# Negated blocks of h made in pieces from SBUF, and a given engine order behind the attention

## The chip, the cores and the metric

The kernel runs on one core of one Trainium2 chip. The metric is the device time of one execution in microseconds; three runs of the kernel before gave 793.66, 793.96 and 795.17, median 793.96. Engines are called as in the profile: PE multiplies matrices, DVE, ACT and POOL do elementwise work, and SP issues most DMA transfers (SPq); POOL issues the DMA transfers that add into DRAM.

## The reference

One decoder layer on 16 meta tokens and 1024 tokens, width 1024, all in fp32:

```python
h = rmsnorm(x, norm_g)                        # x with the meta tokens ahead: 1040 rows
u_pool, z_pool, q, k, v, z_attn, f_logit, g_pool, g_attn = split(h @ w_in)
y_pool = causal_multiscale_pool(u_pool, pool_w, pool_scale) * silu(z_pool)
y_attn = forgetting_attention(q, k, v, log_sigmoid(f_logit + b_forget)) * silu(z_attn)
merged = sigmoid(g_pool) * (y_pool @ w_up_pool) + sigmoid(g_attn) * (y_attn @ w_up_attn)
out = rmsnorm(x + merged @ w_out, final_norm_g)     # meta rows dropped
```

Attention has 8 heads of 64, causal, with a decay by the running sum of the log forget gates. Pooling has four groups of 128 channels with trailing means over 2, 4, 8 and 16 positions.

## The kernel before

**Precision.** Each fp32 operand is split into a high and a low part (`hh` and `hl` of h, `whi` and `wlo` of weights): ACT copies the high part, DVE or POOL subtracts it. A product is three matmuls: high by high, low by high, high by low.

**Stages** (times of the profiled execution, about): norm, transposes and the first projections to 54 us, gates to 88; sixteen attention units (four pairs of heads, two heads each, two halves of the queries) to 513; seven products for the gates z (0 to 6, `g_prod`, L932) from 527 to 620; the up projections (L164 again) to 707; the output product (L1148) to the end.

**In the attention** PE also computes the remaining projections in chunks of 128 columns of `w_in` (`split_w`, `w_chunk`, L164). A chunk's weights, 512 KB, are loaded by SP into a tile "raw" of pool `wp` (L145), which holds two such tiles in turn; ACT copies `whi` (L150), POOL subtracts `wlo` (L152). PE takes its instructions in a written order, so a chunk that is not ready holds up everything behind it.

**Sums for the products.** The two gates z take seven products of 512-blocks instead of eight (a Strassen-like scheme), from sums of weight blocks (GS) and of blocks of h (HS), and the output product takes sums TD of w_out. They are made in DRAM while attention runs, by the table `SUMS`: behind unit i stands a list of steps. `put` is a plain DMA on SP, `add` an adding DMA on POOL's queue. `put_neg` (L590 to L595) makes the negative of a block of h: in two halves it loads the block from DRAM into tiles "neg" *of the ring "raw"*, ACT negates them there (L594), and SP stores them (L595).

**Behind the attention** the products take turns in two sets of four PSUM banks (`ga_`, `gb_`). Their operands are loaded by `w_in_` (weights, tiles "graw") and `h_in` (blocks of h, "hraw") and split by `w_split` (ACT and POOL, L912 and L136) and `h_split` (ACT and DVE, L921 to L925). `keep` copies a bank (ACT), `plus_` adds a bank to what is there (DVE, L947) and applies silu (ACT, L944). Between them lie `pool_chain` (running sums of the pooling, DVE, from a tile "u" loaded from DRAM), `pool_split` (tiles plh and pll), `attn_in` (the attention's output y from DRAM), `attn_norm` (L841 and L842: reciprocal sums "rc" broadcast from DRAM, y times rc) and `pool_mm` (the small matmuls of pooling). Here PE's order is written by hand, while ACT, DVE, POOL and SP get theirs from the scheduler. Pool `gp` holds 13 tiles "g" in rotation: u, its running sums, plh, pll, y and rc all come from it, and a tile's first writer waits for the last reader of what lay in that place.

Of the kernel before, what the change touches and what calls it, by code (L numbers as in the profile page):

```python
# [54 lines left out]
def tile_hybrid_block(ctx, tc, x, meta, norm_g, w_in, b_forget, pool_w, pool_scale,  # L55
# [344 lines left out]
    grow = ap_.tile([1, D], F32, name="grow", tag="t")  # L400
# [166 lines left out]
    HS = {n: dr.tile([512, 512], F32, name=f"hs{n}") for n in ("11", "12", "21", "22", "n12", "n21", "A", "B", "C", "X")}  # L567
# [22 lines left out]
    def put_neg(n):  # L590
        for k in range(2):
            t = wp.tile([128, 2, 512], F32, name="neg", tag="raw")
            put(t, rows_of(HS[n])[:, 2 * k:2 * k + 2])
            after(nc.scalar.activation(t, t, AF.Copy, scale=-1.0), exps[-1])  # L594
            nc.sync.dma_start(rows_of(HS["n" + n])[:, 2 * k:2 * k + 2], t)  # L595

    SUMS = {
        0: [(put_h, "21"), (put_h, "12")],
        1: [(add_h, "21"), (put, GS[1], GB["11"])],
        2: [(add_h, "12"), (put, GS[3], GB["12"])],  # L600
        3: [(put_neg, "21"), (add, GS[1], GB["12"])],
        4: [(put, TD[1], WB["11"]), (put, TD[3], WB["12"]), (add, GS[3], GB["22"])],
        5: [(put_neg, "12"), (put_h, "11")],
        6: [(add, TD[1], WB["12"]), (add_h, "11"), (put, GS[2], GS[3])],
        7: [(add, TD[3], WB["22"]), (put_h, "22"), (put, HS["X"], HS["n21"])],
        8: [(add_h, "22"), (add, rows_of(HS["X"]), rows_of(HS["11"]))],
        9: [(put, TD[2], TD[3]), (put, HS["A"], HS["22"]), (add, GS[2], GB["11"])],
        10: [(add, TD[2], WB["11"]), (add, rows_of(HS["A"]), rows_of(HS["n21"]))],
        11: [(put, HS["B"], HS["A"]), (put, GS[4], GS[2])],
        12: [(put, TD[4], TD[2]), (add, rows_of(HS["B"]), rows_of(HS["11"])), (add, GS[4], GB["21"])],  # L610
        13: [(add, TD[4], WB["21"]), (put, HS["C"], HS["B"])],
        14: [(add, rows_of(HS["C"]), rows_of(HS["n12"]))],
# [203 lines left out]
    def pool_mm(g):  # L816
# [3 lines left out]
        for c0, c1 in HALVES:  # L820
# [31 lines left out]
    def pool_chain(g):  # L852
# [7 lines left out]
        while step < win:  # L860
# [6 lines left out]
            i += 1  # L867
# [85 lines left out]
    for p in range(3):  # L953
        attn_in(p)
# [313 lines left out]
```

## Time and profile before

| What | us |
|---|---|
| median of three runs | 793.96 |
| the profiled execution, as timed | 793.09 |
| its span in the trace | 791.4 |
| PE busy in the span | 730.7 |
| mean granted clock of PE (share of full) | 0.968 |

All rows shown below are of this one execution. "Idle before" is the time in which an engine stood still before a group of instructions, with what ended it; waits of an engine that is not the limit cost nothing. The granted clock is the share of its full clock at which PE was allowed to run in a stretch.

### The profile page before, as it was taken

What the parts mean: (1) busy time and instruction counts of PE and PEld (TensorE: products, weight loads), DVE (VectorE), ACT (ScalarE), POOL (GpSimd) and SP (SyncE); (2) the same over time, 40 slices, a digit from 0 to 9 for tenths busy, and PEclk for the clock granted to TensorE, in tenths of its full rate; (3) what the DMA queues carried; (4) which work ended last, traced back from release to release, by engine and by line L of the source; (5) the groups of instructions that cost most, each with busy time, mean ns of one, the idle gap of its engine ahead of it and who ended that gap; (6) DMA issues with size and microseconds to landing.
All of it is one profiled execution on the core that took longest, in us unless ns stands there. A gap on an engine that the chain in (4) does not pass through costs nothing.

```text
span 791.4 us, 10759 instructions
## 1 busy us (share of the span) xinstructions
PE 730.7 (92%) x3637; PEld 620.7 (78%) x3637; DVE 554.0 (70%) x1023; ACT 398.3 (50%) x814; POOL 340.2 (43%) x404
## 2 busy tenths in 40 slices
PE   8999999997498849998899998997899999999996
PEld 6988899985397648897888876785688888888885
DVE  5643788797189648798887886945548845687774
ACT  7744555555255535575465643524457522524354
POOL 5331238462315245654274645733678401004343
PEclk9999999999599979999999999999799999999999
DMA  9111127918910794847928877289740536764005
GB/s 299 41 28 46 45 83 192 253 33 184 263 35 15 212 263 98 231 91 180 198 64 212 216 179 187 62 276 315 216 147 16 224 107 234 257 241 133 0 1 213
DMA packets 91241, 120.44 MB, mean 152 GB/s; under 512 B 11041, under 2 KB 54049, under 8 KB 91058
## 3 DMA queue, kind: packets, MB, share of 16 engines
q1 hardware_dynamic: 81440, 100.36, 40.4%
q0 software_dynamic: 8448, 16.78, 12.6%
q10 hardware_dynamic: 1298, 2.63, 0.9%
q8 instruction: 28, 0.46, 0.2%
q14 instruction: 27, 0.22, 0.1%
HBM read 92.28 MB, written 52.63 MB: 183 GB/s over the span
## 4 chain that ended last, share of the span: by engine, by line
PE 68%; DMA 9%; DVE 8%; ACT 5%; issue 3%; POOL 1%; SPq 0%; POOLq 0%; DVEq 0%; ACTq 0%
PE pj L164 41%; PE pj L1148 8%; PE pj L932 7%; PE po L718 3%; DMA raw<-in_w_in_dram 3%; PE pt L932 2%; PE pt L1148 2%; DMA hsn<-neg 2%; PE ps L657 2%; PE ps L658 2%; ACT S L666 1%; DVE pl L702 1%; DVE m L673 1%; DMA rc<-recs 1%; DMA sp_u<-st 1%
## 5 line engine op out<-in xcount | busy, mean ns | idle before, releaser
L164 PE MATMUL pj<-hh,whi 128*128 128x512 f32 (+3 forms) x640 | 149.1, 360 | 31.8 <-ACT whi L150 28.7
L164 PEld LDWEIGHTS pj<-hh,whi 128*128 128x128 f32 x640 | 110.2, 192 | 45.2 <-ACT whi L150 29.6
L164 PE MATMUL pj<-hl,whi 128*128 128x512 f32 (+3 forms) x640 | 145.5, 354 | 0.0
L152 POOL TENSOR_TENSOR wlo<-raw,whi 128x256 fp32r<-128x256 f32 x116 | 92.7, 886 | 119.3 <-ACT whi L150 61.7
L164 PE MATMUL pj<-hh,wlo 128*128 128x512 f32 (+3 forms) x640 | 143.0, 350 | 0.0
L164 PEld LDWEIGHTS pj<-hl,whi 128*128 128x128 f32 x640 | 109.8, 191 | 12.1
L164 PEld LDWEIGHTS pj<-hh,wlo 128*128 128x128 f32 x640 | 108.4, 188 | 11.9
L702 DVE TENSOR_TENSOR pl<-S,ph 128x512 fp32r<-128x512 f32 (+4 forms) x112 | 88.6, 806 | 15.5 <-ACT ph L701 14.9
L710 POOL TENSOR_TENSOR acc<-acc,S 128x272 f32<-128x272 f32 (+4 forms) x80 | 76.1, 952 | 13.6 <-ACT S L698 8.9
L666 ACT ACTIVATE S<-ps,negc 128x400 f32<-128x400 f32 (+2 forms) x96 | 49.1, 517 | 57.4 <-DVE S L664 54.9
L136 POOL TENSOR_TENSOR gw<-graw,gw 128x256 fp32r<-128x256 f32 x48 | 50.6, 1089 | 39.6 <-ACT gw L912 17.2
L673 DVE TENSOR_TENSOR m<-m,S 128x272 f32<-128x272 f32 (+4 forms) x80 | 48.0, 601 | 26.8 <-ACT S L666 25.3
L698 ACT ACTIVATE S<-S 128x512 f32<-128x512 f32 (+4 forms) x112 | 49.7, 479 | 31.4 <-DVE S L697 31.2
L150 ACT ACTIVATE whi<-raw 128x512 fp32r<-128x512 f32 x58 | 34.2, 623 | 41.0 <-DMA raw<-in_w_in_dram 28.9
L701 ACT ACTIVATE ph<-S 128x512 fp32r<-128x512 f32 (+4 forms) x112 | 51.9, 479 | 1.8 <-PE po L718 1.4
L932 PE MATMUL pj<-gh,gw 128*128 128x512 f32 x180 | 45.8, 411 | 7.5 <-ACT gh L921 6.1
L697 DVE TENSOR_TENSOR S<-S,pt 128x512 f32<-128x512 f32 (+4 forms) x112 | 51.5, 496 | 0.8
L932 PEld LDWEIGHTS pj<-gh,gw 128*128 128x128 f32 x180 | 35.6, 200 | 16.8 <-ACT gh L921 7.3
L657 PE MATMUL ps<-qa,ka 128*128 128x512 f32 (+4 forms) x112 | 38.8, 347 | 7.8 <-ACT S L666 7.3
L1040 DVE TENSOR_TENSOR rl<-pj,rl 128x512 f32<-128x512 f32 x32 | 22.1, 689 | 31.3 <-PE pj L164 31.3
L718 PE MATMUL po<-pl,V 128*128 128x512 f32 (+4 forms) x112 | 38.7, 345 | 3.6 <-DVE pl L702 3.4
L658 PE MATMUL ps<-ql,ka 128*128 128x512 f32 (+4 forms) x112 | 38.3, 342 | 0.0
(227 smaller groups left out, 1325.9 us busy)
## 6 DMA issues: line engine op xcount, KB each, us to landing
raw<-in_w_in_dram SPq DMA_DIRECT2D x31, 512.0 KB, 6.2
xt<-in_x_dram SPq DMA_DIRECT2D x8, 512.0 KB, 6.7
hs<-hh SPq DMA_DIRECT2D x4, 1024.0 KB, 8.6
hs<-hl POOLq DMA_DIRECT2D x4, 1024.0 KB, 10.5
sp_gp<-st SPq DMA_DIRECT2D x16, 256.0 KB, 4.4
gs<-in_w_in_dram POOLq DMA_DIRECT2D x4, 1024.0 KB, 11.5
td<-in_w_out_dram POOLq DMA_DIRECT2D x4, 1024.0 KB, 10.9
sp_ga<-st SPq DMA_DIRECT2D x16, 256.0 KB, 2.7
```

The costliest lines, as they stand in the source:

```text
L152: ins = nc.gpsimd.tensor_tensor(lo[:, k:k + 2], raw[:, k:k + 2], r32(hi[:, k:k + 2]), op=ALU.subtract)
L164: nc.tensor.matmul(ps, a, b, start=(i == 0), stop=(i == len(seq) - 1))
L657: nc.tensor.matmul(ps[:kb, c0:], ka[:, k0:k0 + kb], qa[:, q0 + c0:q0 + 512], start=True, stop=False)
L658: nc.tensor.matmul(ps[:kb, c0:], ka[:, k0:k0 + kb], ql[:, q0 + c0:q0 + 512], start=False, stop=True)
L666: nc.scalar.activation(s[:kb, f0:], ps[:kb, f0:], AF.Identity, bias=nb_)
L673: nc.vector.tensor_tensor(m[:kb, c0:], m[:kb, c0:], s[:kb, c0:], op=ALU.max)
L701: nc.scalar.activation(ph[:kb, c0:], s[:kb, c0:], AF.Copy)
L702: dves.append(nc.vector.tensor_tensor(pl[:kb, c0:], s[:kb, c0:], r32(ph[:kb, c0:]), op=ALU.subtract))
L710: accs.append(nc.gpsimd.tensor_tensor(acc[:kb, c0:], acc[:kb, c0:], s[:kb, c0:], op=ALU.add))
L718: nc.tensor.matmul(self.po[:, c0:], v, r[:kb, c0:], start=(b == 0 and i == 0), stop=(b == self.nb - 1 and i == 1))
L932: nc.tensor.matmul(ps, op_w[n][p][k // 2][:, k % 2, i * 128:(i + 1) * 128], op_h[n][q][k // 2][:, k % 2], start=start and m == 0, stop=m = ...
L1148: nc.tensor.matmul(ps, pick(A_, k, p)[:, i * 128:(i + 1) * 128], pick(B_, k, q)[:, c0:c1], start=start and n == 0, stop=n == 11, skip_grou ...
```

## The change

**Negated blocks.** `put_neg` works on pieces of 128x512. ACT writes the negated high part of a piece of h from SBUF into a tile "neg" of pool `ap_` (one buffer of its own), POOL subtracts the low part from it in two halves, and SP stores it into the sums that begin with it: block 21 into X and A, block 12 into C. One piece stands behind each of units 0 to 3 (21) and 5 to 8 (12). The DRAM blocks 12, 21 and their negatives are no longer made, X, A and C need one addition each less, and the other sums move by some units.

**Behind the attention** a second manual schedule (`M2`) also gives ACT, DVE and POOL their order, as written; SP stays with the scheduler. The weights of product 2 load into two tiles of `gp`; `pool_chain` is a generator whose steps stand between others; `w_split` does one half at a time; `h_split` does both high parts, then both low parts; silu stands apart from `plus_`. Lastly the row of norm gains moves to pool `gp`, and the low part of pooling group 1 from POOL to DVE.

```diff
-    grow = ap_.tile([1, D], F32, name="grow", tag="t")
+    grow = gp.tile([1, D], F32, name="grow", tag="g")
...
-    def put_neg(n):
-        for k in range(2):
-            t = wp.tile([128, 2, 512], F32, name="neg", tag="raw")
-            put(t, rows_of(HS[n])[:, 2 * k:2 * k + 2])
-            after(nc.scalar.activation(t, t, AF.Copy, scale=-1.0), exps[-1])
-            nc.sync.dma_start(rows_of(HS["n" + n])[:, 2 * k:2 * k + 2], t)
+    def put_neg(blk, k, *dsts):
+        t = ap_.tile([128, 512], F32, name="neg")
+        after(nc.scalar.activation(t, hblock(hh4, blk)[:, k], AF.Copy, scale=-1.0), exps[-1])
+        for c in range(0, 512, 256):
+            sub = nc.gpsimd.tensor_tensor(t[:, c:c + 256], t[:, c:c + 256], hblock(hl4, blk)[:, k, c:c + 256],
+                                          op=ALU.subtract)
+            after(sub, accs[-1])
+        for d in dsts:
+            put(HS[d][128 * k:128 * k + 128], t)
+
+    def n21(k):
+        put_neg("21", k, "X", "A")
+
+    def n12(k):
+        put_neg("12", k, "C")
+
+    def add_s(d, n):
+        add(rows_of(HS[d]), rows_of(HS[n]))
 
     SUMS = {
-        0: [(put_h, "21"), (put_h, "12")],
...
-        3: [(put_neg, "21"), (add, GS[1], GB["12"])],
-        4: [(put, TD[1], WB["11"]), (put, TD[3], WB["12"]), (add, GS[3], GB["22"])],
-        5: [(put_neg, "12"), (put_h, "11")],
...
-        13: [(add, TD[4], WB["21"]), (put, HS["C"], HS["B"])],
-        14: [(add, rows_of(HS["C"]), rows_of(HS["n12"]))],
+        0: [(n21, 0), (put_h, "11")],
...
+        9: [(put, TD[2], TD[3]), (add_s, "C", "B")],
...
+        13: [(add, TD[4], WB["21"])],
+        14: [(add, GS[4], GB["21"])],
     }
...
-            if g:
+            if g > 1:
                 pool_tt(yl[:, c0:c1], zp[g][:, c0:c1], r32(yh[:, c0:c1]), ALU.subtract)
...
-        pool, tag = (hq, "w") if n in (4, 6) else (wp, "raw")
+        pool, tag = {2: (gp, "g"), 4: (0, "w"), 6: (0, "w")}.get(n, (wp, "raw"))
+        pool = pool or hq
...
+    M2 = ExitStack()
+    M2.enter_context(tc.manual_schedule(engines={mybir.EngineType.PE, mybir.EngineType.Activation,
+                                                 mybir.EngineType.DVE, mybir.EngineType.Pool}))
...
+    attn_norm(0)
+    attn_in(2)
+
+    prods(gb_, 3, True)
+    for k in range(2):
+        w_split(4, k)
+    h_split(4)
...
+    prods(ga_, 5, False, (3, 2, 1, 0))
+    for k in range(2):
+        w_split(6, k)
+    h_split(6)
+    plus_(zp[3][:, T0_], gb_[3])
+    silu(zp[3][:, T0_], zp[3][:, T0_], -1.0)
+    pool_split(0)
     for i in range(4):
-        g_prod(gb_[i], 4, i, False)
-        plus_(zp[i][:, T0_], gb_[i], -1.0)
+        silu(za[i][:, T0_], za[i][:, T0_])
     attn_norm(3)
...
+    for i in (3, 2, 1):
+        plus_(zp[i][:, T1_], ga_[i])
+        silu(zp[i][:, T1_], zp[i][:, T1_], -1.0)
...
     ws[0, 0] = up_weights(0, 0)
-    ws[1, 0] = up_weights(1, 0)
+    plus_(zp[0][:, T1_], ga_[0])
+    silu(zp[0][:, T1_], zp[0][:, T1_], -1.0)
     for i in range(4):
         pool_mm(3 - i)
         g_prod(ga_[i], 6, i, False)
```

The order on three places. Numbers in tile names are buffers; a program's own, not the same in both.

SP around units 2 and 3 of the attention, before: `raw` are weight loads, `sums` and `sp_y` stores at the end of a unit, `hs21` the block in DRAM and `hsn21` its negative.

```order
L732 DMA sums_766<-sr_2310 128x16
L337 DMA sp_gp1_2204<-st_2264 128x512
L579 DMA neg_2313<-hs21_782 128x2x512
L727 DMA sp_y0_768<-t_2304 64x512
L579 DMA neg_2317<-hs21_782 128x2x512
L884 DMA fin_5614<-sums_766 32x16x16
L595 DMA hsn21_785<-neg_2313 128x2x512
L337 DMA sp_gp1_2204<-st_2342 128x512
L595 DMA hsn21_785<-neg_2317 128x2x512
L145 DMA raw_2345<-in_w_in_dram 128x8x128
L579 DMA td1_772<-in_w_out_dram 512x512
L145 DMA raw_2510<-in_w_in_dram 128x8x128
```

The same place now:

```order
L579 DMA hsX_787<-neg_2059 128x512
L579 DMA hsA_784<-neg_2059 128x512
L579 DMA hs22_783<-hh1_121 128x4x512
L145 DMA raw_2358<-in_w_in_dram 128x8x128
L744 DMA sums_766<-sr_2056 128x16
L739 DMA sp_y0_768<-t_2050 64x512
L145 DMA raw_2523<-in_w_in_dram 128x8x128
L337 DMA sp_gp0_2041<-st_2114 128x512
L337 DMA sp_gp0_2041<-st_2183 128x512
L145 DMA raw_2712<-in_w_in_dram 128x8x128
L744 DMA sums_766<-sr_2324 128x16
```

The chunk loaded into raw_2345 before is the one loaded into raw_2358 now, and raw_2510 is raw_2523: both stood behind the `sums` store of unit 3 (sr_2310) and the stores of the negative. Now raw_2523 stands ahead of the store of unit 3 (sr_2324), and raw_2358 even ahead of that of unit 2 (sr_2056).

DVE around product 6, before: L842 is y times rc (here of pair 3), L925 a low part of a block of h, L947 an addition of a bank to z, L1019 the low part of up weights, L823 the scaling behind `pool_mm`.

```order
L842 TENSOR_TENSOR y_5803<-y_5803,rc_5985 128x1024
L925 TENSOR_TENSOR gh_5923<-hraw_5899,gh_5921 128x1024
...
L925 TENSOR_TENSOR gh_6021<-hraw_5997,gh_6019 128x1024
L947 TENSOR_TENSOR zp_5796<-pt_5504,zp_5796 128x512
L875 TENSOR_TENSOR pll_5990<-u_5509,plh_5989 128x1024
L925 TENSOR_TENSOR gh_6022<-hraw_5998,gh_6020 128x1024
L875 TENSOR_TENSOR pll_5994<-u_5518,plh_5993 128x1024
L947 TENSOR_TENSOR zp_5782<-pj_5503,zp_5782 128x512
L1019 TENSOR_TENSOR wlu_6100<-rawu_6097,whu_6099 128x512
L947 TENSOR_TENSOR zp_5768<-pj_5502,zp_5768 128x512
L947 TENSOR_TENSOR zp_5754<-pj_5501,zp_5754 128x512
L823 SCALAR_TENSOR_TENSOR zp_5796<-pj_6105,psc_117,zp_5796 128x512
```

The same place now (L854, L941, L962, L1068, L835 are those lines of the new program):

```order
L854 TENSOR_TENSOR y_5825<-y_5825,rc_6016 128x1024
L941 TENSOR_TENSOR gh_6084<-hraw_6002,gh_6082 128x1024
L941 TENSOR_TENSOR gh_6085<-hraw_6003,gh_6083 128x1024
L962 TENSOR_TENSOR zp_5535<-pt_5527,zp_5535 128x512
L889 TENSOR_TENSOR pll_6093<-u_5915,plh_6092 128x1024
L854 TENSOR_TENSOR y_5926<-y_5926,rc_6100 128x1024
L962 TENSOR_TENSOR zp_5535<-pt_5523,zp_5535 128x512
L962 TENSOR_TENSOR zp_5533<-pj_5522,zp_5533 128x512
L962 TENSOR_TENSOR zp_5531<-pj_5521,zp_5531 128x512
L1068 TENSOR_TENSOR wlu_6113<-rawu_6110,whu_6112 128x512
L962 TENSOR_TENSOR zp_5529<-pj_5520,zp_5529 128x512
L835 SCALAR_TENSOR_TENSOR zp_5535<-pj_6120,psc_117,zp_5535 128x512
```

The normalization of pair 3 (rc_5985, now rc_6100) stood ahead of the low parts for product 5, and stands now right ahead of the four additions that empty the banks of that product (pt_5523, pj_5522, pj_5521, pj_5520). PE's first matmul of product 6 writes the bank pj_5520 and waits for the last of them. The load of rc_6100 waits in the new program for the small matmul `pj_6128<-pll_5906`, the second half of `pool_mm(3)`.

SP at the same time, now: the loads of rc, of the operands of products 5 and 6 (graw, hraw), of y and of up weights (rawu).

```order
L914 DMA graw_5897<-gs3_778 128x2x512
L914 DMA graw_5898<-gs3_778 128x2x512
L853 DMA rc_5821<-recs_767 64x1024 x2
L846 DMA y_5825<-sp_y2_770 128x1024
...
L853 DMA rc_5922<-recs_767 64x1024 x2
L846 DMA y_5926<-sp_y3_771 128x1024
L914 DMA hraw_6003<-hs22_783 128x2x512
L1064 DMA rawu_6110<-in_w_up_pool_dram 128x4x128
L1064 DMA rawu_6242<-in_w_up_pool_dram 128x4x128
L853 DMA rc_6016<-recs_767 64x1024 x2
L853 DMA rc_6100<-recs_767 64x1024 x2
```

Before, the four loads of rc stood behind y of pair 3 and beside the operands of products 3 to 5; the first of them stands now behind the weights of product 5 (graw from gs3), and the last two behind everything that product 6 loads.

More of the change, by code (lines that the diff above doesn't have):

```diff
@@ L566, in tile_hybrid_block @@
           for r in range(2) for c, col in enumerate((COL_ZA, COL_Z))}
[L567 removed]
+    HS = {n: dr.tile([512, 512], F32, name=f"hs{n}") for n in ("11", "12", "21", "22", "A", "B", "C", "X")}
     accs = []
@@ L944, in silu, with plus_, prods @@
         evacs.append(nc.scalar.activation(z, ps, AF.Silu, scale=scale))
-    def plus_(dst, ps, scale):
+    def plus_(dst, ps):
         nc.vector.tensor_tensor(dst, ps, dst, op=ALU.add)
-        silu(dst, dst, scale)
-    pool_chain(3)
-    pool_chain(2)
+    def prods(ps, n, start, order=range(4)):
+        for i in order:
+            g_prod(ps[i], n, i, start)
+    for i in range(4):
+        za[i], zp[i] = btile("za"), btile("zp")
+    cg = {g: pool_chain(g) for g in range(4)}
     w_in_(1)
-    for p in range(3):
-        attn_in(p)
```

146 lines of the change are left out of this document (82 added, 64 removed).

## The prediction

> **What bounds the kernel now.** First the page, for which engine is the limit, and for the clock it was granted:
>
> ```profile
> PE 730.7 (92%) x3637; PEld 620.7 (78%) x3637; DVE 554.0 (70%) x1023; ACT 398.3 (50%) x814; POOL 340.2 (43%) x404
> PEclk9999999999599979999999999999799999999999
> ```
>
> PE is busy for 730.7 of 791.4 us, so time is only to be had where PE stands idle (about 61 us in all) or runs below its full clock: slices 11, 15 and 28, around 200, 285 and 545 us. The view of waits on PE says for whom it stood:
>
> ```profile
> engine line waited for: us in total, times, longest us
> PE pj L164 <- ACT whi L150: 28.7, 2, 17.2
> PE ps L657 <- ACT S L666: 7.3, 8, 2.6
> PE pj L932 <- ACT gh L921: 6.1, 2, 5.7
> ```
>
> The first row is two stalls of projections whose weights had not been split yet. The chain of waits shows what the split waited for; columns are start, length, what:
>
> ```profile
> 192.88 0.95 ACT neg L594
> 193.86 3.46 DMA hsn<-neg
> 197.38 11.14 DMA raw<-in_w_in_dram
> 209.23 1.65 PE pj L164 x3
> ...
> 266.68 1.07 ACT neg L594
> 267.76 9.74 DMA hsn<-neg
> 277.57 8.70 DMA raw<-in_w_in_dram
> 286.97 1.97 PE pj L164 x5
> ```
>
> Both times it reads: ACT negates a block in the ring of raw weights, the store of it must end, and only then is the weight load issued into the same ring; PE resumes when that load has landed and been split. The ring, not the arithmetic, is the limit here. The stretches behind the stalls, and those of the later losses (length; busy time and instructions of PE, PEld, DVE, ACT, POOL; granted clock; DMA share; GB/s):
>
> ```profile
> 192.00:209.20 17.20, 0.07 (x1) 0.00 (x0) 1.78 (x3) 4.02 (x8) 2.74 (x4) 0.58 1.02 256
> 209.20:215.40 6.20, 6.17 (x15) 4.82 (x16) 0.91 (x1) 2.81 (x5) 4.84 (x7) 0.50 1.05 311
> 287.00:290.50 3.50, 3.50 (x12) 3.50 (x13) 0.00 (x0) 2.07 (x4) 3.49 (x6) 0.51 1.18 393
> 478.00:485.10 7.10, 4.50 (x15) 3.14 (x13) 2.70 (x5) 4.12 (x7) 5.76 (x7) 0.76 1.10 306
> 548.80:564.00 15.20, 7.66 (x18) 5.16 (x18) 12.41 (x10) 8.14 (x10) 11.31 (x8) 0.66 0.66 187
> 564.00:620.40 56.40, 56.40 (x249) 46.52 (x249) 36.17 (x35) 33.72 (x46) 40.01 (x36) 1.00 0.44 138
> ```
>
> After a stall PE works at half clock for some us (0.50 for 6.2 us, 0.51 for 3.5). The last row is the undisturbed products: 56.40 us for 249 matmuls, 0.2265 us each.
>
> **Part 1: the two stalls go.** In the new program the raw loads of these two places stand on SP ahead of, or between, short stores of finished pieces, and nothing but raw weights uses the ring. A chunk of projection keeps PE for some 16 us (72 matmuls of 0.2265, three products by 8 contraction blocks by 3 column pieces of at most 512), and a load now has that long to land; the slowest above took 11.14 us, beside two other large transfers. Gain: 28.7 us of waits; half of 6.2 us, 3.1; 0.49 of 3.5 us, 1.7; and a small wait where ACT was held up by the negation of a whole 128x1024:
>
> ```profile
> 268.36 0.50 PE L657 MATMUL ps<-qa,ka 128*128 128x512 f32 x1 [0.83 <-ACT S L666]
> ```
>
> 0.8 us, so 28.7 + 3.1 + 1.7 + 0.8 = **34.3 us**.
>
> [...]
>
> **Part 2: the new pieces.** Eight pieces, one in each of units 0 to 3 and 5 to 8. The rows nearest to their work, and the whole stretch of the attention:
>
> ```profile
> L150 ACT ACTIVATE whi<-raw 128x512 fp32r<-128x512 f32 x58 | 34.2, 623 | 41.0 <-DMA raw<-in_w_in_dram 28.9 <-PE pj L164 11.2 <-issue 0.8
> L152 POOL TENSOR_TENSOR wlo<-raw,whi 128x256 fp32r<-128x256 f32 x116 | 92.7, 886 | 119.3 <-ACT whi L150 61.7 <-PE pj L164 25.1 <-PE po L718 10.9
> 88.00:513.00 425.00, 382.06 (x1918) 329.75 (x1916) 328.18 (x678) 222.33 (x503) 209.73 (x237) 0.96 0.61 153
> 190.04 0.28 POOL L707 COPY acc<-S 128x112 f32<-128x112 f32 x1 [11.25 <-ACT S L698]
> ```
>
> ACT pays 8 x 0.62 = 5.0 us, less the four negations of about 1 us each that go (0.95 and 1.07 in the chain); POOL pays 16 x 0.89 = 14.2 us. ACT is idle for 203 and POOL for 215 of the 425 us, POOL in pieces like the 11.25 us of the last row, at the end of every unit, which is where the pieces are put. The row nearest to them is therefore that wait, and I take **0**. The upper end, if nothing covered them, is 5.0 - 4.0 + 14.2 = 15 us; below zero only by the DMA traffic saved, which no PE row waits for by itself.
>
> The sums move by one to six units. One late wait lies among them, of 2.6 us (second row of the waits), with its clock loss: in 478.00:485.10, 15 matmuls in 7.1 us. There the first block of ACT's raw weights for the products is loaded beside a 1 MB copy of HS C from B. The copy is moved to an addition at unit 9, while additions at units 13 and 14 stay. Gain between 0 and 4.3 us (2.6 and half of 3.4); nearest to the row that stays, **1**. The other edits (the row of norm gains in another pool, group 1's low part from POOL to DVE) touch nothing that PE waits for: 0, and under 1 us if DVE is late there.
>
> **Part 3: behind the attention.** PE's order is the same; the order of ACT, DVE and POOL is now given. Before, all that is lost here is lost in 548.80:564.00: 15.2 us for 18 matmuls, which would take 4.1, so **11.1 us** lost. The rows:
>
> ```profile
> 554.50 1.22 PE L932 MATMUL pj<-gh,gw 128*128 128x512 f32 x2 [5.69 <-ACT gh L921]
> 559.64 8.88 PE L932 MATMUL pj<-gh,gw 128*128 128x512 f32 x30 [1.42 <-DVE gh L922]
> 552.68 11.53 POOL L136 TENSOR_TENSOR gw<-graw,gw 128x256 fp32r<-128x256 f32 x8 [12.37 <-ACT gw L912]
> L921 ACT ACTIVATE gh<-hraw 128x1024 fp32r<-128x1024 f32 x2 | 2.1, 1040 | 0.0
> L922 DVE SCALAR_TENSOR_TENSOR gh<-hraw,gh 128x1024 fp32r<-128x1024 f32 x2 | 3.5, 1756 | 0.0
> L925 DVE TENSOR_TENSOR gh<-hraw,gh 128x1024 fp32r<-128x1024 f32 x8 | 13.3, 1673 | 10.5 <-ACT gh L924 10.5
> ```
>
> The order given to DVE and the waits of the program leave these waits after the change. (a) Product 2: the second high part of its h block can be written only when product 1 has ended, then the low part follows on DVE: 1.04 + 1.76 us less the matmuls that need neither, 1.1 us: 1.7. (b) Product 4: the normalization of pair 0 stands ahead of the low part of h. Its reciprocals are loaded on SP behind the weights of product 5, into slots that POOL frees by splitting the weights of product 3; it begins about 4.3 us after product 1's end (behind ACT's four high parts) and took 11.5 us in the third row. So the reciprocals are issued 16 us after that end and land 22 to 25.5 us after it (6 to 8.7 us); product 4 could begin at 1.7 + 2 x 10.9 = 23.5. Then come 1.23 us and 1.67 for each low part, of which the first is needed 0.9 us in: 0.5 to 5 lost, 2.5 taken. (c) Product 5, the same with pair 1: 0 to 1.2, 0.6 taken. (d) Product 6. The reciprocals of pair 3 go into the slot of the low part of pooling group 3, which is read for the last time by the small matmuls *behind product 5*. So SP issues the load there; DVE's normalization waits for it, and stands ahead of the four additions that empty the banks of product 5, whose last lets product 6 begin. PE has nothing in between. The rows:
>
> ```profile
> rc<-recs SPq DMA_DIRECT2D x8, 256.0 KB, 8.7
> rawu<-in_w_up_pool_dram SPq DMA_DIRECT2D x4, 256.0 KB, 2.8
> 566.40 1.23 DVE L842 TENSOR_TENSOR y<-y,rc 128x1024 f32<-128x1024 f32 x1 [3.47 <-issue]
> L947 DVE TENSOR_TENSOR zp<-pj,zp 128x512 f32<-128x512 f32 x6 | 4.0, 682 | 1.1 <-PE pj L932 1.1
> L944 ACT ACTIVATE zp<-zp 128x512 f32<-128x512 f32 x8 | 5.0, 626 | 5.1 <-DVE zp L947 5.1
> L1018 ACT ACTIVATE whu<-rawu 128x512 fp32r<-128x512 f32 x2 | 1.3, 627 | 3.4 <-DMA rawu<-in_w_up_pool_dram 3.4
> L1019 DVE TENSOR_TENSOR wlu<-rawu,whu 128x512 fp32r<-128x512 f32 x2 | 1.5, 732 | 2.4 <-ACT whu L1018 2.4
> ```
>
> Landing 2.8 (that size on an empty queue) to 8.7 us (beside other loads); it will be two of them and nothing else, so I take 5.0 from first issue. Then 1.23, three additions 2.05, on ACT the last silu 0.63 and the high part of the up weights 0.63, their low part on DVE 0.73, the last addition 0.68: 5.0 + 5.95 = 11.0 us (8.8 to 14.7). The clock loss behind a stall of that length was 1.7 and 3.1 above: 2.4.
>
> Sum after: 1.7 + 2.5 + 0.6 + 11.0 + 2.4 = 18.2 us, with bounds of 13 (1.7 + 0.5 + 0 + 8.8 + 1.7) and 26 (1.7 + 5 + 1.2 + 14.7 + 3.1). Against 11.1 before the tail **loses 7.1 us** (2 to 15).
>
> **Sum.** The profiled execution took 793.1 us. 793.1 - 34.3 - 1.0 + 0 + 7.1 = 764.9. The median of the runs, 793.96, lies 0.9 above it, so the forecast is **765.8 us**.
>
> **Rivals.** *The tail does not pay (18%).* For (d) the load need not be the last to come if I have misread which tile the slot is freed by, or it lands in under 3 us and the additions overlap better than one behind the other. Without (d), 13.4 us are saved: 752.4; with half of it, 759. Against it: the order is explicit, and PE's next instruction is the one that waits.
>
> *DVE takes over in the attention (15%).* When the stalls go, 425 us become about 390 for the same 328 us of DVE, a share of 0.84 instead of 0.77, and it is higher inside:
>
> ```profile
> 220.00:265.00 45.00, 42.96 (x217) 36.62 (x216) 40.37 (x87) 27.32 (x60) 18.48 (x22) 1.00 0.11 28
> ```
>
> DVE is busy for 0.90 there while PE still is for 0.95. If POOL's 14.2 us of new subtractions each hold up DVE and that holds up PE, the time is 765.8 + 14.2 = 780. Against it: PE waited for DVE only briefly in the attention, and most subtractions fall where POOL waits for the exponentials. [...]
>
> *Slower (5%): the pieces' stores block SP.* The raw loads stand on SP behind stores of pieces that wait for POOL's subtraction, which waits for the unit's exponentials. If that comes later than the 16 us of cover, a load is as late as before, not twice but in up to eight units. One such stall costs 11.5 + 1.7 = 13.2 us; with 765.8, three of them give 805, slower than before, and two 792. It decides from the third unit on. *It does not do what it says (3%):* the DMA share of 1.02 in 192.00:209.20 means the transfers, not the ring, made the load late; the stalls stay and the tail pays: 793.96 + 7.1 = 801. Against both: the neg loads and stores themselves made much of that traffic and go.
>
> **How the numbers follow.** Forecast 59%, tail cheap 18%, DVE 15%, slower ones 8%. The range 752 to 782 takes in the first three with their bounds (the upper one: 780, and the tail's +8 with part of the DVE case); outside are the slower ones and a few per cent below. A measurement of this kernel tells 0.2%, 1.6 us, from no change. Faster 0.90, within that bound 0.03 (the DVE case with the dear tail), slower 0.07.
>
> **What would show it.** Right: no wait of PE on L150's split above 3 us, no slice of PEclk under 9 near 200 and 285; a wait of PE before product 6 of about 11 us whose releaser is a DVE addition (after's L962), with a load of rc ending some 6 us before it. Wrong: that wait is missing or short (tail cheap); DVE or ACT releases PE in many units of the attention (DVE takes over); the raw loads are issued late again behind SP's stores of pieces (slower).

## The result, and the profile after

| | us, median (lowest to highest) | against before, ratio [95%] |
|---|---|---|
| before, measured again beside it | 793.81 (793.00 to 795.17) | |
| after | 784.46 (783.33 to 785.86) | 0.9881 [0.9860, 0.9903] |
| forecast | 765.8 (range 752 to 782) | |

The change makes the kernel 1.2% faster. The forecast was 3.5%: the sign was right, the size was not, and the time lies 2.5 us above the range. The profiled execution after took 785.86 us, with a span of 783.8. The page of after first; its lines answer to those of before:

```profile
PE 735.2 (94%) x3637; PEld 624.6 (80%) x3637; DVE 567.7 (72%) x1025; ACT 397.9 (51%) x818; POOL 342.0 (44%) x414
PEclk9999999998998999999999999999997999999999
```

The two gaps in the clock near 200 and 285 us are gone. DVE, which has two instructions more to run (1025, before 1023), is busy for 13.7 us more (567.7, before 554.0): a first sign. The view of waits on PE after:

```profile
PE ps L669 <- ACT S L678: 10.9, 11, 2.7
PE pj L947 <- DVE zp L962: 10.1, 1, 10.1
PE po L730 <- DVE pl L714: 10.0, 8, 4.3
PE pt L947 <- DVE gh L941: 3.0, 2, 2.6
```

Nothing waits for the split of L150 any more (28.7 us before). In its place stand three others: ACT's copies of the scores, which empty the bank that PE writes next (10.9, before 7.3), the low part of the exponentials on DVE (10.0 at L714; before, 3.4 at L702), and one of 10.1 us for an addition on DVE, before product 6.

To see where the time went, the span is cut into stages: from the first matmul of the scores to the first of the products (attention), and from there to the last of the products. The view of stretches, with length, busy time and instructions of PE, PEld, DVE, ACT, POOL, then granted clock, DMA share and GB/s; of before:

```profile
82.30:526.60 444.30, 401.23 (x2015) 345.94 (x2014) 342.73 (x703) 230.10 (x519) 211.39 (x239) 0.96 0.61 154
526.60:620.00 93.40, 85.86 (x360) 69.19 (x359) 54.74 (x50) 48.16 (x65) 62.08 (x58) 0.95 0.59 184
```

and of after:

```profile
83.90:510.30 426.40, 402.88 (x2013) 348.71 (x2012) 352.91 (x696) 229.82 (x523) 228.41 (x259) 0.97 0.58 143
510.30:612.90 102.60, 87.46 (x361) 69.29 (x360) 56.43 (x56) 45.99 (x62) 49.25 (x49) 0.93 0.50 160
```

The attention gained 17.9 us where 35.3 were forecast (34.3 of stalls and 1.0); the products lost 9.2 where 7.1 were forecast. What comes after is alike (171.4 and 170.9 us to the end). The attention starts 1.6 us later in this one execution; the other runs below, whose code ahead of it is nearly the same, start at most 0.9 us later than before, so I take that part for chance. 17.4 + 2.1 + 1.6 - 0.1 (the rest) = 21.0 us is what the profiled time has over the 764.9 of the sum. **So the question is where 17.4 us of the attention went.**

Added up over PE's timeline, before lost 42.5 us there in waits and 8.3 by half clock, after 23.1 and 11.0: the gain is still about what the stages show (16.6 of 17.9), and new losses stand in after. The largest, in the timeline of after at unit 3 (start, length, engine, what; in brackets the idle time before it, and what ended it):

```profile
181.63 5.53 DVE L683 TENSOR_TENSOR m<-S 128x400 f32<-128x400 f32 x1 [0.56 <-ACT S L678]
181.68 1.91 POOL L594 TENSOR_TENSOR neg<-neg,hl 128x256 f32<-128x256 f32 x2
183.78 3.95 POOL L152 TENSOR_TENSOR wlo<-raw,whi 128x256 fp32r<-128x256 f32 x4
187.09 1.08 DVE L714 TENSOR_TENSOR pl<-S,ph 128x400 fp32r<-128x400 f32 x1
188.22 0.70 PE L730 MATMUL po<-pl,V 128*128 128x400 f32 x1 [4.29 <-DVE pl L714]
```

One DVE operation of 128x400 took 5.53 us. It began 0.05 us before POOL's first subtraction of the new piece, and ended 0.57 us before the end of the four subtractions of a weight chunk that follow on POOL: POOL worked through six instructions of 128x256 nearly without a break (it issued one adding DMA between them), and DVE stood in its operation meanwhile. PE waited 4.29 us for what is next on DVE, and then had half clock (0.50 for 6.8 us). The same happens in unit 1 at 133 us, with a wait of 2.15 us.

Is this DVE operation always so slow? The groups of L714 and of L709 on DVE in after (shortest, median and longest, in ns; the second operand of L709, pt, lies in PSUM, both of L714 in SBUF):

```profile
L714 DVE TENSOR_TENSOR pl<-S,ph x112: 158/730/4694, 99.4 to 492.1; 128x512 fp32r<-128x512 f32 x48, 128x400 fp32r<-128x400 f32 x16, 128x272 fp32r<-128x272 f32 x16, 128x144 fp32r<-128x144 f32 x16
L709 DVE TENSOR_TENSOR S<-S,pt x112: 156/561/691, 95.2 to 486.5; 128x512 f32<-128x512 f32 x48, 128x400 f32<-128x400 f32 x16, 128x272 f32<-128x272 f32 x16, 128x144 f32<-128x144 f32 x16
```

Same shapes, same engine, same counts: with one operand in PSUM the longest is 691 ns, with two in SBUF it is 4694. And the trace of before had shown it already, in the same two groups:

```profile
L702 DVE TENSOR_TENSOR pl<-S,ph x112: 158/718/4009, 97.9 to 508.4; 128x512 fp32r<-128x512 f32 x48, 128x400 fp32r<-128x400 f32 x16, 128x272 fp32r<-128x272 f32 x16, 128x144 fp32r<-128x144 f32 x16
L697 DVE TENSOR_TENSOR S<-S,pt x112: 152/560/691, 93.7 to 502.8; 128x512 f32<-128x512 f32 x48, 128x400 f32<-128x400 f32 x16, 128x272 f32<-128x272 f32 x16, 128x144 f32<-128x144 f32 x16
```

The prediction shows neither row. Beside the 4009 ns of L702, from 454.34 us of before on, POOL made four weight subtractions (L152, 454.75 to 457.91).

Product 6 went much as the prediction has it. The timeline of after from the last small matmul of product 5 on (SPq: issue of the two halves of rc):

```profile
585.66 1.08 SPq L853 DMA_DIRECT2D rc<-recs  x2
590.28 1.22 DVE L854 TENSOR_TENSOR y<-y,rc 128x1024 f32<-128x1024 f32 x1 [3.69 <-DMA rc<-recs]
591.42 0.68 DVE L962 TENSOR_TENSOR zp<-pt,zp 128x512 f32<-128x512 f32 x1
592.02 1.28 DVE L962 TENSOR_TENSOR zp<-pj,zp 128x512 f32<-128x512 f32 x2
594.51 0.69 DVE L1068 TENSOR_TENSOR wlu<-rawu,whu 128x512 fp32r<-128x512 f32 x1 [1.22 <-ACT whu L1067]
595.12 0.68 DVE L962 TENSOR_TENSOR zp<-pj,zp 128x512 f32<-128x512 f32 x1
595.96 1.62 PE L947 MATMUL pj<-gh,gw 128*128 128x512 f32 x3 [10.10 <-DVE zp L962]
```

From the issue to DVE's start 4.6 us, then 5.7 us until PE goes on.

### The profile page after: what moved, and what is told of

The parts are those of the page before. It is cut to its first block, busy times and chain, and to the rows that moved or that the text cites. A ratio compares the mean times of both kernels' runs of the same rounds, so it can differ in the third digit from the quotient of the medians.

```text
span 783.8 us, 10785 instructions
## 1 busy us (share of the span) xinstructions
PE 735.2 (94%) x3637; PEld 624.6 (80%) x3637; DVE 567.7 (72%) x1025; ACT 397.9 (51%) x818; POOL 342.0 (44%) x414
## 3 DMA queue, kind: packets, MB, share of 16 engines
q0 software_dynamic: 7392, 14.68, 11.6%
## 4 chain that ended last, share of the span: by engine, by line
PE 68%; DVE 13%; ACT 5%; issue 4%; DMA 4%; SPq 0%; POOLq 0%; DVEq 0%; ACTq 0%; POOL 0%
PE pj L164 42%; PE pj L1202 8%; PE pj L947 6%; DVE pl L714 4%; PE po L730 3%; PE pt L1202 2%; PE pt L947 2%; DMA rc<-recs 2%; PE ps L669 2%; PE ps L670 2%; DVE S L709 2%; ACT S L678 1%; PE pj L509 1%; ACT ph L713 1%; DVE ka L278 1%
## 5 line engine op out<-in xcount | busy, mean ns | idle before, releaser
L164 PE MATMUL pj<-hl,whi 128*128 128x512 f32 (+3 forms) x640 | 147.9, 358 | 0.0
L164 PE MATMUL pj<-hh,wlo 128*128 128x512 f32 (+3 forms) x640 | 144.7, 353 | 0.3 <-POOL wlo L428 0.3
L152 POOL TENSOR_TENSOR wlo<-raw,whi 128x256 fp32r<-128x256 f32 x116 | 96.7, 936 | 97.6 <-ACT whi L150 42.1
L164 PEld LDWEIGHTS pj<-hl,whi 128*128 128x128 f32 x640 | 111.4, 194 | 12.4
L714 DVE TENSOR_TENSOR pl<-S,ph 128x512 fp32r<-128x512 f32 (+4 forms) x112 | 94.6, 858 | 15.4 <-ACT ph L713 14.2
L136 POOL TENSOR_TENSOR gw<-graw,gw 128x256 fp32r<-128x256 f32 x48 | 48.2, 1040 | 40.5 <-ACT gw L928 35.9
L685 DVE TENSOR_TENSOR m<-m,S 128x272 f32<-128x272 f32 (+4 forms) x80 | 50.3, 629 | 17.5 <-ACT S L678 15.5
L947 PE MATMUL pj<-gh,gw 128*128 128x512 f32 x180 | 45.6, 407 | 12.1 <-DVE zp L962 10.1
L947 PEld LDWEIGHTS pj<-gh,gw 128*128 128x128 f32 x180 | 35.0, 198 | 22.0 <-issue 10.5
L709 DVE TENSOR_TENSOR S<-S,pt 128x512 f32<-128x512 f32 (+4 forms) x112 | 51.7, 497 | 0.8
L730 PE MATMUL po<-pl,V 128*128 128x512 f32 (+4 forms) x112 | 39.4, 352 | 10.2 <-DVE pl L714 10.0
L669 PE MATMUL ps<-qa,ka 128*128 128x512 f32 (+4 forms) x112 | 37.7, 337 | 11.2 <-ACT S L678 10.9
L720 POOL TENSOR_TENSOR acc<-S 128x400 f32<-128x400 f32 (+1 forms) x16 | 20.5, 1280 | 47.9 <-ACT S L710 47.7
L150 ACT ACTIVATE whi<-raw 128x512 fp32r<-128x512 f32 x58 | 34.3, 623 | 13.7 <-PE pj L164 10.5
```

The source lines that it names most:

```text
L152: ins = nc.gpsimd.tensor_tensor(lo[:, k:k + 2], raw[:, k:k + 2], r32(hi[:, k:k + 2]), op=ALU.subtract)
L164: nc.tensor.matmul(ps, a, b, start=(i == 0), stop=(i == len(seq) - 1))
L669: nc.tensor.matmul(ps[:kb, c0:], ka[:, k0:k0 + kb], qa[:, q0 + c0:q0 + 512], start=True, stop=False)
L685: nc.vector.tensor_tensor(m[:kb, c0:], m[:kb, c0:], s[:kb, c0:], op=ALU.max)
L709: nc.vector.tensor_tensor(s[:kb, c0:], s[:kb, c0:], self.pm[:kb, c0:], op=ALU.subtract)
L714: dves.append(nc.vector.tensor_tensor(pl[:kb, c0:], s[:kb, c0:], r32(ph[:kb, c0:]), op=ALU.subtract))
```

## The experiments

The theory, from the 5.53 us of L683 and from L714 against L709 (4694 and 691 ns): DVE operations with two operands in SBUF are held up while POOL works without a break; the new subtractions make POOL's rows longer, and PE waits at the end of them. Rivals: the loss comes from the rest of the new pieces (the one buffer, ACT's new work, the stores); or from the tail reaching back; or the gain of the stalls was overstated. Line numbers differ a little from kernel to kernel.

| Kernel | us | ratio [95%] | attention | products |
|---|---|---|---|---|
| before | 793.81 | | 444.3 | 93.4 |
| after | 784.46 | 0.9881 [0.9860, 0.9903] | 426.4 | 102.6 |
| e1_att | 775.59 | 0.9756 [0.9722, 0.9790] | 427.3 | 93.9 |
| e2_tail | 802.80 | 1.0120 [1.0085, 1.0155] | 444.7 | 102.5 |
| e4_dve | 775.86 | 0.9775 [0.9742, 0.9808] | 417.5 | 102.0 |
| e5_nosub | 773.56 | 0.9758 [0.9698, 0.9818] | 416.5 | 99.6 |
| e9_dose | 798.03 | 1.0053 [1.0036, 1.0070] | 440.2 | 101.2 |
| e3_rc3 | 778.68 | 0.9796 [0.9773, 0.9819] | 427.0 | 97.0 |
| e7_fix6 | 774.84 | 0.9760 [0.9738, 0.9781] | 427.1 | 91.9 |
| e10_best | 766.46 | 0.9656 [0.9633, 0.9678] | 418.1 | 93.8 |
| e13_order | 764.16 | 0.9624 [0.9606, 0.9643] | 418.1 | 91.0 |
| e14_neg2 | 763.07 | 0.9621 [0.9602, 0.9640] | 416.4 | 89.5 |

Of the four runs of e5_nosub one took 782.75 us and the others 771.41 to 773.83, which is why its interval is wide. The stages are those of one execution each.

**The halves of the change apart.** e1_att is before with the new pieces and sums, and with the order behind the attention left to the scheduler; e2_tail is before with the given order and the other edits behind the attention. Their core:

```diff
 e1_att, against after
...
-    M2.enter_context(tc.manual_schedule(engines={mybir.EngineType.PE, mybir.EngineType.Activation,
-                                                 mybir.EngineType.DVE, mybir.EngineType.Pool}))
...
 e2_tail, against after
...
-    def put_neg(blk, k, *dsts):
+    def put_neg(n):
+        for k in range(2):
+            t = wp.tile([128, 2, 512], F32, name="neg", tag="raw")
...
```

> The new pieces, sums and place of the row of norm gains, with the scheduler's order behind the attention as before. If the two parts add up, this is the changed kernel without what its tail loses (9.2 us from the first product to the up projections): 784.5 - 9.2 = 775, PE without the 10 us wait before product 6, but with the waits at 137 and 184 us. If the tail's loss comes from the new attention and not from the given order, it stays near 784.

> The kernel before with the given order behind the attention alone. If the parts add up: 794 + 9.2 = 803, with both stalls of before and the wait of about 10 us before product 6. If the loss there came with the new attention: 794.

The attention's half saves 18.4 us of the 793.95 measured beside it, the order behind it costs 8.4 (against 794.41); together 10.0, and the whole change saves 9.35. The halves add up, so each loss can be looked for in its own half. The waits of 2.17 and 4.30 us for L714 are in e1_att as in after; the tail has no part in them.

**The subtraction moved to DVE, and left out.** e4_dve subtracts the low part on DVE in one operation of 128x512 (POOL 16 instructions fewer, DVE 8 more). e5_nosub leaves the subtraction of the low part out, so the negated pieces carry the high part alone.

```diff
 e4_dve (e5_nosub: only the lines with -)
-        for c in range(0, 512, 256):
-            sub = nc.gpsimd.tensor_tensor(t[:, c:c + 256], t[:, c:c + 256], hblock(hl4, blk)[:, k, c:c + 256],
-                                          op=ALU.subtract)
-            after(sub, accs[-1])
+        after(nc.vector.tensor_tensor(t, t, hblock(hl4, blk)[:, k], op=ALU.subtract), dves[-1])
```

> The changed kernel with the low part of each piece subtracted on DVE in one 128x512 operation instead of on POOL in two halves. If DVE is held up by POOL's unbroken rows of operations (theory: lock), the waits of 2.2 and 4.3 us at 137 and 184 us and their half clock go, 11 us, and DVE's own 8 x 0.7 us are mostly covered: 774 to 777. If DVE is simply full once the stalls are gone (rival), its 5.5 us more make it slower: 785 to 790. If the losses are only chance alignments (rival): 782 to 787.

> The changed kernel without the subtraction of the low part (left out: the negated blocks are the high part alone). Lock: 11 us less and no DVE cost, 772 to 775, no DVE operation near POOL's six in a row over 4 us long in units 1 and 3. Full DVE: the same or little less, 780 to 784, since DVE does the same work. Chance: 782 to 787.

Without POOL's subtraction the kernel is 10.9 us faster, and with the same work on DVE 8.6 us faster, although DVE is the engine that PE waited for and got 8 x 0.68 = 5.5 us of work more. Both lie in the ranges expected for the theory. The timeline of e4_dve shows the operation that took 5.53 us in after:

```profile
179.06 0.57 DVE L680 TENSOR_TENSOR m<-S 128x400 f32<-128x400 f32 x1 [0.56 <-ACT S L675]
```

and the view of its groups the new ones (shortest, median, longest in ns):

```profile
L593 DVE TENSOR_TENSOR neg<-neg,hl x8: 679/682/687, 108.1 to 309.8; 128x512 f32<-128x512 f32 x8
```

It takes 0.57 us again. Both gains are net. By PE's timelines the waits at units 1 and 3 with their clock loss, 11.0 us in after, are 1.0 us in e4_dve and 0.4 in e5_nosub; the rest of the piece (ACT's copy, the buffer, the stores) is the same in e4_dve, so this rival is not where these 11 us are. Besides them e4_dve lost less near 310 us (0.95 us of wait, after 4.0 and 1.7 of half clock), and has a new wait of 2.43 us with 2.8 of half clock at 338 us: there a DVE operation of 128x272 took 2.75 us, until just behind the end of four weight subtractions on POOL. What of after's loss stays without the subtraction is in the timeline of PE in e5_nosub:

```profile
149.56 0.50 PE L665 MATMUL ps<-qa,ka 128*128 128x512 f32 x1 [2.40 <-ACT S L674]
302.04 0.65 PE L665 MATMUL ps<-qa,ka 128*128 128x512 f32 x1 [2.91 <-ACT S L674]
```

Two waits for ACT, 5.3 us, which before did not have. In both places ACT itself had just waited, 2.49 and 2.82 us by the trace of e5_nosub, until the piece in its one buffer had been stored. The same chain in the timeline of after:

```profile
299.16 0.34 SPq L744 DMA_DIRECT2D sums<-sr  x1
306.41 0.32 SPq L898 DMA_DIRECT2D fin<-sums  x1
307.88 0.54 SPq L579 DMA_DIRECT2D hsC<-neg  x1
310.63 0.63 ACT L592 ACTIVATE neg<-hh 128x512 f32<-128x512 f32 x1 [2.35 <-DMA hsC<-neg]
312.38 0.50 PE L669 MATMUL ps<-qa,ka 128*128 128x512 f32 x1 [2.70 <-ACT S L678]
```

ACT wants to write the next piece, and its only buffer is still to be stored. The store was issued at 307.88, some 14 us after POOL had finished that piece at 294.0. Ahead of it on SP stand the stores of the unit's end and, before them, a load of the attention's sums (`fin`): SP stood at that load for 6.9 us, until the store of the sums issued at 299.16 had landed. In ACT's order the copies of the scores that PE waits for stand behind the piece. This is a second, smaller loss of the pieces, and it is the rival of the buffer.

**More of the suspected cause.** e9_dose does each half three times on POOL (subtract, add, subtract), six instructions a piece instead of two.

```diff
-            sub = nc.gpsimd.tensor_tensor(t[:, c:c + 256], t[:, c:c + 256], hblock(hl4, blk)[:, k, c:c + 256],
-                                          op=ALU.subtract)
-            after(sub, accs[-1])
+            for op in (ALU.subtract, ALU.add, ALU.subtract):
+                sub = nc.gpsimd.tensor_tensor(t[:, c:c + 256], t[:, c:c + 256], hblock(hl4, blk)[:, k, c:c + 256],
+                                              op=op)
+                after(sub, accs[-1])
```

> The changed kernel with each half of the low part subtracted, added and subtracted again on POOL: six operations for a piece instead of two, to the same value but for rounding. Lock: DVE's operations near 134 and 181 us, 4.7 and 5.5 us long behind rows of six, lie behind rows of ten and get some 3 to 4 us longer each, PE's waits there too, and other units get such waits: 792 to 800. If POOL's own load or DVE's being full is the cause, nothing of PE's waits follows the row's length, and the time stays within 3 us of 784.5.

13.6 us slower than after, all of it in the attention (440.2, after 426.4), where POOL is still busy for only 252 of 440 us. The timeline of e9_dose at unit 1, and its waits on PE:

```profile
132.90 8.29 DVE L715 TENSOR_TENSOR pl<-S,ph 128x272 fp32r<-128x272 f32 x2
133.68 4.63 POOL L595 TENSOR_TENSOR neg<-neg,hl 128x256 f32<-128x256 f32 x6
```

```profile
PE ps L670 <- ACT S L679: 16.4, 15, 4.1
PE po L731 <- DVE pl L715: 16.4, 10, 6.8
```

The two DVE operations took 5.59 us together in after, and take 8.29 here. The first is the same in both (0.98 and 0.96); the second, of 128x144, took 4.69 us beside six POOL instructions and takes 7.40 beside ten, where most of its shape take 0.30. At unit 3 POOL issues a DMA between its six and its four, and DVE got one turn there: two operations took 5.34 and 3.66 us, one behind the other. PE's waits in the two units are 4.85 and 6.78 us, 2.7 and 2.5 more than in after; the expectation had 3 to 4 more. In all, the wait for L715 grows by 6.4 us, that for ACT by 5.5; how much of the second is DVE's delay handed on and how much the buffer, which is freed later here, these rows don't part.

**The wait before product 6.** e3_rc3 moves the normalization of pair 3 behind the last addition. e7_fix6 puts all four additions first on DVE, ahead of `pool_split(0)`, the silus and the up weights, and the normalization behind the second of the four groups of product 6.

```diff
 e3_rc3
-    attn_norm(3)
     for i in (3, 2, 1):
...
     silu(zp[0][:, T1_], zp[0][:, T1_], -1.0)
+    attn_norm(3)
 e7_fix6
+    for i in (3, 2, 1, 0):
+        plus_(zp[i][:, T1_], ga_[i])
+        silu(zp[i][:, T1_], zp[i][:, T1_], -1.0)
     pool_split(0)
     for i in range(4):
         silu(za[i][:, T0_], za[i][:, T0_])
-    attn_norm(3)
-    for i in (3, 2, 1):
-        plus_(zp[i][:, T1_], ga_[i])
-        silu(zp[i][:, T1_], zp[i][:, T1_], -1.0)
...
+        if i == 1:
+            attn_norm(3)
```

> The changed kernel with the normalization of pair 3 moved behind the additions that empty the banks of product 5. If the wait before product 6 is the chain over the load of the reciprocals, it goes with its half clock: 10.1 + 2.1 = 12 us, 772. If the additions and silus themselves are late (rival), some 4 us of wait stay: 777 to 780.

> The changed kernel with another order of DVE and ACT around product 6: the four additions that empty the banks of product 5 first, then the last split of the pooling, the up weights, and the normalization of pair 3 only behind the second matmuls of pooling. Where only the normalization was moved, 6.5 us of wait stayed, for the split, the up weights and the additions behind them. If that is all, the wait before product 6 is under 1 us and the time 784.5 - 10.1 - 2.1 = 772. If a further wait comes up (the high part of the last pooling group, or the reciprocals behind product 6), 775 to 779.

e3_rc3 misses its 772: 5.8 us are gained, not 12. With the normalization out of the way, the next in DVE's order is late. From its timeline:

```profile
583.70 1.52 DVE L889 TENSOR_TENSOR pll<-u,plh 128x1024 fp32r<-128x1024 f32 x1 [1.64 <-ACT plh L888]
588.23 0.69 DVE L1067 TENSOR_TENSOR wlu<-rawu,whu 128x512 fp32r<-128x512 f32 x1 [1.22 <-ACT whu L1066]
588.84 0.68 DVE L962 TENSOR_TENSOR zp<-pj,zp 128x512 f32<-128x512 f32 x1
589.67 1.62 PE L947 MATMUL pj<-gh,gw 128*128 128x512 f32 x3 [6.50 <-DVE zp L962]
```

The pooling's low part and that of the up weights stand ahead of the last addition too, and both wait for ACT. In e7_fix6, with the additions first, the wait is gone, but one of 1.85 us comes later (for L835), so it took 774.84 and not 772; its products take 91.9 us, less than before's 93.4.

**Together.** e10_best joins e4_dve and e7_fix6 and moves the normalizations of pairs 0 and 1 behind `h_split` of products 4 and 5. e13_order moves them on: pair 1 to where pair 2 was (behind product 4's additions), pairs 2 and 3 into product 6. e14_neg2 is e13_order with two buffers for the pieces (and `HROW` 1056 instead of 1088 to make room).

```diff
 e13_order, beside the edits of e4_dve and e7_fix6
-    attn_norm(0)
     attn_in(2)
...
     h_split(4)
+    attn_norm(0)
...
-    attn_norm(1)
     attn_in(3)
...
-    attn_norm(2)
+    attn_norm(1)
...
+        if i in (1, 2):
+            attn_norm(i + 1)
```

> The low part of the pieces on DVE, the order around product 6 of the kernel that changes that alone, and the normalizations of pairs 0 and 1 moved behind the low parts of the blocks of h for products 4 and 5. If the three losses add up: 775.9 - 12.2 - about 4 (the waits of 0.9, 0.4, 2.6 and 0.4 us before products 4 and 5, and half of a half-clock stretch of 3.4) = 759 to 761. If what is freed shows the next wait (the blocks of h themselves), 763 to 768.

> The low part of the pieces on DVE, and all four normalizations off the way of the products: pair 0 behind the low parts for product 4, pair 1 behind the additions behind product 4, pairs 2 and 3 behind the second and third matmuls of pooling. The kernel with the pieces on DVE took 775.9; the order around product 6 alone brought 9.6, the waits of 0.9 and 0.4 us before product 4 should go too: 764 to 766. If a load of reciprocals again stands ahead of something PE needs, a wait of several us shows before product 6, and 768 to 772.

> The same with two buffers for the pieces in turn (room made by rows of h of 1056 instead of 1088 elements). With one buffer ACT's copy of a piece waits until the piece before has been stored, and that store waits on SP behind other transfers: PE's waits at 150 and 301 us (1.1 and 0.7 us in the kernel with the pieces on DVE; 2.7 at 310 in the changed kernel) should go, 2 to 4 us: 761 to 764. If they come from elsewhere, no change (within 1.5 us); the other pitch of h could move it either way by as much.

e10_best falls short of its 759 to 761 and lies in its second range. Its timeline has a wait before product 6 again, and the chain to it begins with the normalization of pair 1 (L851), which in its new place waits for its load:

```profile
562.91 1.22 DVE L851 TENSOR_TENSOR y<-y,rc 128x1024 f32<-128x1024 f32 x1 [1.93 <-DMA rc<-recs]
565.91 1.83 ACT L956 ACTIVATE zp<-zp 128x512 f32<-128x512 f32 x3 [10.81 <-DVE zp L959]
567.64 1.99 ACT L925 ACTIVATE gw<-graw 128x1024 fp32r<-128x1024 f32 x2
569.54 1.99 ACT L933 ACTIVATE gh<-hraw 128x1024 fp32r<-128x1024 f32 x2
570.61 3.38 DVE L938 TENSOR_TENSOR gh<-hraw,gh 128x1024 fp32r<-128x1024 f32 x2 [0.67 <-ACT gh L933]
577.13 1.19 PE L944 MATMUL pj<-gh,gw 128*128 128x512 f32 x2 [4.85 <-ACT zp L956]
```

Behind it in DVE's order stand a part of the pooling and the additions of product 4; ACT's silus (L956) wait for these and stand ahead of the split of product 6's operands (L925, L933); DVE's low parts (L938) wait for that, and the additions that empty the banks of product 5 come behind them. In e13_order, where pair 1 stands behind the additions and pair 2 in product 6, the wait is 1.44 us.

e13_order and e14_neg2 came as expected and beat both kernels: 764.16 and 763.07 us, 2.6% under after. They can't be told from each other by time, so whether the second buffer pays is not shown by it; PE's waits at 151 and 302 us (1.09 and 0.72) are gone, and one at 148 us is longer by 0.35.

## Why the prediction was off

**Part 1, the stalls: right.** 28.7 us of waits for L150 and the clock losses behind them are gone; e1_att has them away without the tail, and e2_tail has both of them still (29.2 us) without the pieces. By the sums of losses, 50.7 us before less the 35.3 would have left 15.4; after shows 34.1. So 18.7 us are new, or were there and were not seen. The cover of 16 us for a load was reckoned wrong, without harm: a chunk is not 72 matmuls of 512 columns but 48 of 512, or 72 of 384 and 272, in both traces, so 48 x 0.2265 = 10.9 us of PE; the attention's own matmuls between them stretch it (167.3 to 182.2 us in after). And the third dip of the clock is slice 29 of before's page, 554 to 574 us, not 28.

**Part 2, the pieces at 0: this step failed.** It asked only when POOL and ACT had time ("at the end of every unit, which is where the pieces are put"), and POOL had it. It did not ask what DVE does meanwhile. Of the 18.7 us:
- at units 1 and 3, POOL's rows of six: waits of 2.15 and 4.29 us, and the half clock behind them, 1.7 and 2.8: 11.0 us. Shown by e4_dve and e5_nosub, where 1.0 and 0.4 us of it are left, and by e9_dose, where the waits are longer. e1_att, e3_rc3 and e7_fix6, with the same attention, have both waits to within 0.02 us; the half clock behind them costs 4.7, 1.7 and 4.8 us there.
- at 307 to 317 us, 1.34 + 2.70 and 1.7 of half clock: 5.7 us. Of the 2.70 the timeline shows the buffer as the cause; the other wait and the clock behind both are put here by their place alone.
- half clock at 242 to 248 us, 3.1 us, behind the same three short waits which before has too, without such a loss; and 1.7 + 1.7 at 371 us, a wait for ACT whose cause was not traced.
- against these 23.2 us, about 4.5 us net of waits of before near 392 and 480 us and their half clock are gone, beyond the 1 that the sum had taken (a new wait of 2.20 us near 281 us is counted against them).

The upper end of 15 us for this part was worked out as if POOL's time itself were what PE pays. What was paid is of that size, but it hangs on two places where POOL goes on without a break, not on the sum of POOL's work.

**The 1 us for the sums** was too little: the wait of 2.59 us at 481 us and its clock loss are gone, but for small rests.

**Part 3, behind the attention: the chain right, (c) mis-sized, and 2.1 us short.** (d) 10.1 us and 2.1 of clock loss for 11.0 and 2.4; the load took 4.5 us for 5.0. (a) 0.7 for 1.7, (b) 1.3 for 2.5; its upper end of 5 was more than its own terms give (16 + 8.7 + 1.23 + 1.67 - 0.9 less 23.5 is 3.2). (c) was mis-sized: 2.60 and 0.40 us of waits for the low part, with 1.5 of half clock behind them, for 0.6; the load of pair 1 landed 11.6 us after its first issue, where the sum had 8.7 at most. These add up to 18.7, for 18.2; counted as 361 matmuls of 0.2265 us against the stage's 102.6 us it is 20.8, and before, with 360, 11.9. The 2 us between the two counts are spread over the products, and no row names them.

**The rivals.** "DVE takes over" came nearest, with 780, and what it supposes, that POOL's subtractions hold up DVE and that this holds up PE, is what the runs show (5.53 us on DVE and 4.29 on PE in after, 0.57 on DVE in e4_dve); 15% was too little for it. What stood against it in the prediction (PE waits for DVE only briefly, subtractions fall into POOL's pauses) were both true before the change and are no argument: what filled POOL's pauses lengthened DVE's operations there (0.57 us to 5.53 at unit 3). "SP's stores block" did not come true for the weights, whose loads no longer appear among the waits; it did for a piece (307.88 above), at a fifth of its price. "The tail is cheap" and "it doesn't do what it says" did not happen.

**What stays open.** Without the subtraction the attention takes 416.5 us, where the sum had 409.0. The two waits for ACT (5.3 us) are most of that, but e14_neg2 with two buffers has 416.4 against e13_order's 418.1, one execution each, so a second buffer alone brings less than 2; what else delays ACT there was not settled. DVE operations are long beside rows of four weight subtractions on POOL as well: 4.01 us for 128x400 at 454 us of before, 4.00 for the same shape at 441 us of after. Not beside every such row: one of 128x272 took 1.01 us at 181 us of e4_dve. A kernel without these rows was not tried.

## What to carry to other kernels

The work put into POOL's idle time was not free here: 11.0 us of waits and half clock on PE at two units. Before elementwise work goes to POOL, compare on DVE the longest times of an operation with two operands in SBUF with those of the same shapes with one in PSUM (4009 and 691 ns in before), and count how long POOL then works nearly without a break (6.05 us at unit 3 of after). Where an order is given by hand, look along the in-order queue for every instruction that stands ahead of the one that releases PE: when the first is moved away, the next one is late (10.1 us became 6.5, then 1.9). The single buffer between two engines and a DMA queue coupled all three here: the store of a piece that POOL had finished at 294.0 was issued at 307.88, behind what stood ahead of it in the queue; ACT waited 2.35 us for that store, and PE 2.70 for ACT.

## What the runs showed of the hardware

**DVE was held up for a row of POOL instructions, not for one.** An operation of 0.57 us took 5.53 beside six POOL instructions of 128x256; one of 0.30 took 4.69 beside six and 7.40 beside ten. Of the two groups of after above only the one with both operands in SBUF has such times: of 128x512, L714 took 1038 ns on average and L709, with an operand in PSUM, 681; no L709 took over 691, though POOL worked beside some of them (128x400 at 176.10 us of after, beside two weight subtractions of POOL from 176.07 to 177.51: 0.56 us). At units 1 and 3 of after the DVE operation did not end between two POOL instructions, and the one of 5.53 us had begun 0.05 us ahead of POOL's row, by the profile, whose spans on POOL are rough. What ends such an operation is not settled: with a DMA issued between two POOL instructions one ended there at unit 3 of e9_dose (5.34 us, then 3.66) and none at unit 3 of after, and the 1.01 us at 181 us of e4_dve ended within a row of four (180.11 to 184.08) without such a DMA.

**Half clock came in stretches of 3.4, 6.8, 10.2 and 20.5 us.** Four of the seven stretches in which PE worked at half clock in after (same columns as above; the other three are 3.4 us long):

```profile
187.10:193.90 6.80, 5.67 (x16) 4.71 (x17) 5.52 (x17) 2.70 (x10) 0.63 (x1) 0.50 1.13 211
241.70:248.50 6.80, 6.14 (x16) 4.98 (x17) 6.59 (x14) 0.87 (x2) 3.30 (x5) 0.50 0.91 166
572.80:576.20 3.40, 3.00 (x8) 2.34 (x8) 3.40 (x6) 1.20 (x3) 0.00 (x0) 0.50 0.51 128
589.90:600.10 10.20, 4.14 (x10) 3.34 (x11) 5.63 (x8) 4.24 (x7) 2.79 (x4) 0.50 0.09 26
```

They are 3.4, 6.8 and 10.2 us long. Before has such stretches of 20.5 us (194.9 to 215.4) and 10.2 us (280.2 to 290.5) around its two stalls; the 6.2 and 3.5 us in the prediction are the parts of them in which PE worked again. The second stretch of after stands behind waits of 0.97, 0.27 and 0.79 us within 4 us, which before had to within 0.01 us (0.98, 0.27, 0.79) and paid nothing for. e1_att, e7_fix6 and e3_rc3 have them too, with 3.4, 3.4 and no us of half clock behind them. What decides whether such waits are followed by half clock is not shown; the same ones cost 3.1 us in the execution of after and nothing in those of before and e3_rc3.
